# Paired heads of a hybrid attention block: product u is begun only behind the last matmul of product w

## The chip, the cores and the metric

The kernel runs on one core of a Trainium2 chip. The metric is the time on the device of one execution, in microseconds (us). Before the change it is 819.78 us, the median of three runs (819.44 to 820.15).

## What is computed

The reference is one decoder block on 512 tokens with a model width of 2048, in float32. The tokens are normalised and projected; two groups of heads attend in parallel, each head's output is gated, and one output projection and a last norm follow. Cut to what matters here:

```python
h = _rmsnorm(x, norm_g[l])
proj = h @ w_in[l]
(qa, kca, vca, ksa, vsa, kwa, vwa, za, ga, qb, kb, vb, zb) = jnp.split(proj, offsets, axis=-1)
...
o_a = gates[..., 0:1] * o_cmp + gates[..., 1:2] * o_sel + gates[..., 2:3] * o_win
y_a = o_a.reshape(B, S, WIDTH_A) * jax.nn.silu(za)
...
y_b = o_b.reshape(B, S, WIDTH_B) * jax.nn.silu(zb)
x = x + jnp.concatenate([y_a, y_b], axis=-1) @ w_out[l]
```

Group A has 8 heads of 128 (compressed, selected and window attention), group B 16 heads of 64 (a window of 128 with sinks). Each head of group A needs two projections of the same tokens: its query (out of qa) and its gate (out of za), each 2048 by 128.

## The kernel before

**Words.** TensorE multiplies float32 values as two words, a high word (whi, a copy by ScalarE) and a low word (wlo, the rest, a subtraction by VectorE). `mm3` (L121) makes three matmuls of each product: high by high (L122), high by low (L123), low by high (L124). A weight tile of 128 by 1024 is loaded by a DMA on SyncE's queue (raw), split by ScalarE (L634) and by VectorE (L635), and used by TensorE. In `mm3` as `prod` calls it, the third matmul is the first that reads the low words of the weights.

**Stages.** First the key and value projections with the compression of blocks (to about 180 us), then the heads of group A (to about 402 us), then the heads of group B, then the output projection with the norm. The change lies in the second stage.

**Paired heads.** Head 0 of group A is projected directly. For heads 1 to 7, `pair(h)` (L674) computes query and gate together in a scheme of seven products instead of eight: tokens are cut into two halves of 256, rows of the weights into even and odd blocks, and sums of weight tiles meet sums of token forms that were made earlier (`xf`, L621 to L631). The seven products are 22, p, 21, 12, w, u and q, in the order in which the code names them. Each is one call of `prod` (L661): eight blocks of the contraction, three matmuls of 128 by 256 each, so 24 matmuls. Two banks of PSUM take them (tile pj, names pa and pb): pa's first half takes p and then 12 on top, its second half w; pb's first half takes 22 and then 21, its second half u and then q. Between the products VectorE sums weight tiles (raw plus raw, L684 through `plus`), adds products to the running result (t or zr with pj, L684), and ScalarE copies a half out (L700, L706, L712). Once w and u are both added, VectorE turns the query by the rotary tables (L723 to L725), splits it (L486, L487) and attention can use it.

**Attention of a head.** `attn_a` (L534) goes through four blocks of 128 queries. For each a group of score matmuls (six or nine at L557) writes tile sp; sp has one buffer of three banks, so a group waits until VectorE has read the one before (L559, L563). ScalarE takes the exponentials (L569, L573) and scales (L583, L585), TensorE transposes (L595, L607, L609, tile tp, two buffers), the two engines split the result (L525, L526, and L613 to L615 for the last piece), and TensorE multiplies by the values (L601 to L603, L616, L618, tile op). VectorE gates the head's output (L498) and it is written away (tile yd, L500).

**Order.** A planner places the instructions of each engine when the program is built, by its own estimates, keeping data dependences. So the attention of one head and the products of the next are woven together on TensorE, and one engine's queue runs strictly in the built order. `tc.issue_after(i)` adds an order without data: what is named inside stands behind i on i's engine. `pair` uses it once (L697), for the sum of two weight tiles. Between w and u the code before prescribes nothing: they write different halves of different banks and read different weights (u1 and u5).

**Reloads.** At head 3 the keys and values of the second key head are fetched back into the tiles of the first (L764, L766). After head 7 the even blocks of the tokens are fetched back (L642), the rotary tables of group B replace those of group A in the same tiles (L778, L779) and are scaled by VectorE (L780, L781).

Of the kernel before, what the change touches and what calls it, by code (L numbers as in the profile page):

```python
# [35 lines left out]
def hybrid_block(ctx, tc, xT, xtm, w0, w1s, w2s, wz, wq, wkb, wo0, wos, cw1, cw2, cpos, rope, tabs, sinks, gT, fg, out):  # L36
# [34 lines left out]
    last = {}  # L71
# [47 lines left out]
    recent = {}  # L119

    def mm3(ps, ah, al, bh, bl, first, last, go_on=False):  # L121
        pe.matmul(ps, ah, bh, start=first, stop=False, skip_group_check=go_on)  # L122
        pe.matmul(ps, ah, bl, start=False, stop=False, skip_group_check=go_on)  # L123
        recent["mm"] = pe.matmul(ps, al, bh, start=False, stop=last, skip_group_check=go_on).ins  # L124
# [261 lines left out]
    for g in range(2):  # L386
        act.activation(KH[g][:, 0:CMP], kct[:, g * 32:g * 32 + 32], AF.Copy)
        dve.tensor_tensor(out=KL[g][:, 0:CMP], in0=kct[:, g * 32:g * 32 + 32], in1=KH[g][:, 0:CMP].bitcast(F32),
                          op=ALU.subtract)
# [271 lines left out]
    def prod(bank, u, op, new):  # L661
        for m in range(8):
            cs = slice(m * P, m * P + P)
            ah, al = xf[op, m]
            mm3(bank, u[0][:, cs], u[1][:, cs], ah, al, new and m == 0, m == 7, not new)

    tags = ["raw0", "raw1", "raw2", "raw3"]

# [5 lines left out]
    def pair(h, *early):  # L674
# [20 lines left out]
        with ExitStack() as behind:  # L695
            if "jj" in last:
                behind.enter_context(tc.issue_after(last["jj"]))  # L697
            plus(x2, x2, x4)
        prod(pb[:, H0], u0, "22", True)
        act.activation(d, pb[:, H0], AF.Copy, scale=-1.0)  # L700
        x3 = load(c3, 1)
        prod(pa[:, H0], u3, "p", True)
        plus(d, d, pa[:, H0])
        u2 = unit(x3)
        prod(pb[:, H0], u2, "21", False)
        act.activation(zr[:, H1], pb[:, H0], AF.Copy)  # L706
        plus(jj, d, zr[:, H1])
# [672 lines left out]
```

## Time and profile before

| what | before |
|---|---|
| time, median of three | 819.78 us |
| time of the profiled execution | 820.54 us |
| its span, first to last instruction | 818.8 us |
| instructions in it | 14134 |
| TensorE matmul, busy | 805.6 us (98%) |
| TensorE weight load, busy | 733.7 us (90%) |
| VectorE, busy | 666.6 us (81%) |
| ScalarE, busy | 483.6 us (59%) |
| mean granted clock of TensorE | 0.998 |

The profile calls the engines PE (matmul), PEld (weight load), DVE (VectorE), ACT (ScalarE), POOL and SP; a q behind a name is the engine's sequencer. A row of the timeline gives the start and the length in us, the engine, the line, the operation, the tile written and the tiles read, and in square brackets how long the engine had stood idle just before and which instruction ended that. A row of waits reads: who waited, for whom, us in total, how often, the longest. Matmul ends are modelled, so a matmul that waits shows as a hole before its weight load first.

### The profile page before, as it was taken

To read this page: it belongs to the slowest core of one execution; us is meant where nothing else is said; L and a number is where in the kernel's file an instruction comes from. 1 tells how busy PE (TensorE), PEld (TensorE's weight loads), DVE (VectorE), ACT (ScalarE), POOL (GpSimd) and SP (SyncE) were. 2 spreads that over 40 slices of the span, in tenths; PEclk is the share of its full clock that TensorE was granted. 3 is DMA by queue.
4 is the path that set the end of the run, shared out by engine and by line. 5 is a ranking of instruction groups with operands and counts; after the bars stand their busy time and mean duration, and the time that the engine had idled before them with its cause. 6 is when DMAs were issued, how large, how long until landed. Compare 5 with 4: busy or idle time off the path is not lost.

```text
span 818.8 us, 14134 instructions
## 1 busy us (share of the span) xinstructions
PE 805.6 (98%) x5281; PEld 733.7 (90%) x5281; DVE 666.6 (81%) x1326; ACT 483.6 (59%) x1026; POOL 67.7 (8%) x54
## 2 busy tenths in 40 slices
PE   9999999999999999999999999999999999999996
PEld 8888898999999999999988888888888888999996
DVE  7859786966889899899876688887687799777895
ACT  6734456564867687786756365645444657543545
POOL 4500002020000000000011211011001000000000
PEclk9999999999999999999999999999999999999999
DMA  9665786898421322423742422222222257497845
GB/s 327 201 204 168 264 289 226 258 333 306 137 85 33 116 78 93 168 83 99 233 141 68 138 78 55 75 87 69 78 78 77 77 145 260 145 244 205 242 99 205
DMA packets 52116, 128.30 MB, mean 157 GB/s; under 512 B 4944, under 2 KB 17232, under 8 KB 52048
## 3 DMA queue, kind: packets, MB, share of 16 engines
q1 hardware_dynamic: 50032, 120.59, 43.9%
q0 software_dynamic: 1728, 6.29, 4.4%
q8 instruction: 41, 0.67, 0.3%
q10 hardware_dynamic: 288, 0.52, 0.2%
q14 instruction: 27, 0.22, 0.1%
HBM read 110.31 MB, written 17.07 MB: 156 GB/s over the span
## 4 chain that ended last, share of the span: by engine, by line
PE 85%; DVE 5%; DMA 4%; ACT 3%; issue 2%; POOL 1%; SPq 0%; DVEq 0%; ACTq 0%; POOLq 0%
PE pj L124 16%; PE pj L123 16%; PE pj L122 16%; PE bank L124 4%; PE bank L122 4%; PE oa L123 4%; PE bank L123 4%; PE oa L122 4%; PE oa L124 3%; PE sp L557 3%; DMA rw<-wos 2%; PE tp L595 2%; PE tp L879 2%; DMA xr<-xT 1%; PE spb L844 1%
## 5 line engine op out<-in xcount | busy, mean ns | idle before, releaser
L124 PE MATMUL pj<-xh,wlo 128*128 128x512 f32 (+1 forms) x560 | 194.9, 348 | 1.8 <-DVE wlo L635 1.8
L122 PE MATMUL pj<-xh,whi 128*128 128x512 f32 (+1 forms) x560 | 194.7, 348 | 0.0
L123 PE MATMUL pj<-xl,whi 128*128 128x512 f32 (+1 forms) x560 | 194.6, 347 | 0.0
L96 DVE TENSOR_TENSOR wlo<-raw,whi 128x1024 fp32r<-128x1024 f32 (+2 forms) x102 | 116.7, 1148 | 34.8 <-ACT whi L95 29.4
L95 ACT ACTIVATE whi<-raw 128x1024 fp32r<-128x1024 f32 (+1 forms) x101 | 95.0, 943 | 76.9 <-PE pj L123 22.8
L124 PEld LDWEIGHTS pj<-xh,wlo 128*128 128x128 f32 x560 | 105.4, 188 | 15.0 <-DVE wlo L635 2.4
L123 PEld LDWEIGHTS pj<-xl,whi 128*128 128x128 f32 x560 | 105.3, 188 | 13.1 <-issue 0.9
L122 PEld LDWEIGHTS pj<-xh,whi 128*128 128x128 f32 x560 | 105.3, 188 | 12.2
L635 DVE TENSOR_TENSOR wlo<-raw,whi 128x1024 fp32r<-128x1024 f32 x49 | 59.5, 1220 | 9.3 <-ACT whi L634 9.2
L634 ACT ACTIVATE whi<-raw 128x1024 fp32r<-128x1024 f32 x49 | 51.1, 1054 | 21.1 <-DVE raw L684 6.1
L123 PE MATMUL oa<-wlo,yh 128*128 128x256 f32 (+1 forms) x168 | 50.2, 299 | 0.1
L122 PE MATMUL oa<-whi,yh 128*128 128x256 f32 (+1 forms) x168 | 49.8, 298 | 0.6 <-ACT yh L954 0.6
L124 PE MATMUL oa<-whi,yl 128*128 128x256 f32 (+1 forms) x168 | 49.5, 298 | 0.0
L858 ACT ACTIVATE ttb<-ttb,sums 128x256 f32<-128x256 f32 (+1 forms) x64 | 30.1, 471 | 26.5 <-DVE sums L851 26.1
L525 ACT ACTIVATE ph<-tp 128x512 fp32r<-128x512 f32 x56 | 32.4, 592 | 14.9 <-PE tp L595 8.7
L123 PE MATMUL bank<-wlo,xh 128*128 128x256 f32 (+1 forms) x128 | 40.3, 317 | 0.3 <-DVE wlo L96 0.3
L124 PE MATMUL bank<-whi,xl 128*128 128x256 f32 (+1 forms) x128 | 39.9, 314 | 0.0
L526 DVE TENSOR_TENSOR pl<-tp,ph 128x512 fp32r<-128x512 f32 x56 | 37.8, 684 | 1.9 <-ACT ph L525 1.8
L122 PE MATMUL bank<-whi,xh 128*128 128x256 f32 (+1 forms) x128 | 36.7, 318 | 1.5 <-ACT whi L95 1.5
L122 PE MATMUL bank<-xh,whi 128*128 128x512 f32 x96 | 37.3, 400 | 0.0
L123 PE MATMUL bank<-xl,whi 128*128 128x512 f32 x96 | 36.9, 389 | 0.0
L573 ACT ACTIVATE tt<-tt,sums 128x128 f32<-128x128 f32 (+3 forms) x64 | 35.3, 554 | 1.2 <-DVE sums L563 1.2
(359 smaller groups left out, 2172.6 us busy)
## 6 DMA issues: line engine op xcount, KB each, us to landing
raw<-wz SPq DMA_DIRECT2D x36, 512.0 KB, 3.6
raw<-wq SPq DMA_DIRECT2D x28, 512.0 KB, 3.7
raw<-cw SPq DMA_DIRECT2D x16, 512.0 KB, 4.6
raw<-wos SPq DMA_DIRECT2D x12, 512.0 KB, 4.6
rw<-wos SPq DMA_DIRECT2D x10, 512.0 KB, 5.6
xr<-xT SPq DMA_DIRECT2D x16, 256.0 KB, 5.0
raw<-w SPq DMA_DIRECT2D x8, 512.0 KB, 4.5
fd<-ft SPq DMA_DIRECT2D x4, 1024.0 KB, 6.2
```

The lines of the kernel that those rows point to most:

```text
L95: last["hi"] = act.activation(hi[:, :width], rw[:, :width], AF.Copy).ins
L96: last["lo"] = dve.tensor_tensor(out=lo[:, :width], in0=rw[:, :width], in1=hi[:, :width].bitcast(F32), op=ALU.subtract).ins
L122: pe.matmul(ps, ah, bh, start=first, stop=False, skip_group_check=go_on)
L123: pe.matmul(ps, ah, bl, start=False, stop=False, skip_group_check=go_on)
L124: recent["mm"] = pe.matmul(ps, al, bh, start=False, stop=last, skip_group_check=go_on).ins
L525: act.activation(ph, tp, AF.Copy)
L526: dve.tensor_tensor(out=pl, in0=tp, in1=ph.bitcast(F32), op=ALU.subtract)
L557: pe.matmul(sp[:, a:b], qq[:, qs], kk[0][:, ko:ko + b - a], start=pi == 0, stop=pi == 2)
L573: act.activation(tv, tv, AF.Exp, bias=mn[:, i, 1 + w:2 + w], scale=-1.0, accum_out=dn[:, i, 1 + w:2 + w])
L634: act.activation(hi, src, AF.Copy)
L635: last["lo"] = dve.tensor_tensor(out=lo, in0=src, in1=hi.bitcast(F32), op=ALU.subtract).ins
L858: act.activation(tv, tv, AF.Exp, bias=mn[:, e, v:v + 1], scale=-1.0, accum_out=dn[:, e, v:v + 1])
```

## The change

`prod` is the only place changed. While the first block of u is named (its first three matmuls), an order is in force that puts them on TensorE behind the last matmul of w, which `prod` notes down when it has named w. The blocks of u after the first are named outside that order; they add to the same half bank. It holds for the seven calls of `pair`. No tile, buffer, size or operation is changed.

```diff
         for m in range(8):
             cs = slice(m * P, m * P + P)
             ah, al = xf[op, m]
-            mm3(bank, u[0][:, cs], u[1][:, cs], ah, al, new and m == 0, m == 7, not new)
+            with ExitStack() as behind:
+                if m == 0 and op == "u":
+                    behind.enter_context(tc.issue_after(last["w"]))
+                mm3(bank, u[0][:, cs], u[1][:, cs], ah, al, new and m == 0, m == 7, not new)
+        if op == "w":
+            last["w"] = recent["mm"]
```

## The prediction

> **What bounds the kernel now.** I read the page first: busy shares, the slices, the chain that ended last.
>
> ```profile
> span 818.8 us, 14134 instructions
> PE 805.6 (98%) x5281; PEld 733.7 (90%) x5281; DVE 666.6 (81%) x1326; ACT 483.6 (59%) x1026; POOL 67.7 (8%) x54
> ...
> PE   9999999999999999999999999999999999999996
> ...
> PEclk9999999999999999999999999999999999999999
> ...
> PE 85%; DVE 5%; DMA 4%; ACT 3%; issue 2%; POOL 1%; SPq 0%; DVEq 0%; ACTq 0%; POOLq 0%
> ```
>
> TensorE (PE) bounds it, at full clock in every slice. The change keeps the number of matmuls and only moves them, so it can win no more than the time in which TensorE stands still, and only in the stage of the paired heads, where products w and u live. That stage runs from about 205 to 402 us. The view by windows gives the whole stage and two pieces of it.
>
> ```profile
> 205.00:402.00 197.00, 195.17 (x1611) 190.65 (x1611) 179.37 (x398) 147.82 (x364) 0.00 (x0) 1.00 0.33 107
> 308.00:338.00 30.00, 30.00 (x257) 29.80 (x256) 26.94 (x58) 21.82 (x54) 0.00 (x0) 1.00 0.46 160
> 338.00:368.00 30.00, 29.04 (x241) 28.32 (x241) 27.17 (x60) 23.71 (x59) 0.00 (x0) 1.00 0.19 62
> ```
>
> Columns: stretch, length, then busy time and count for PE, PEld (weight loads), DVE (VectorE), ACT (ScalarE). 257 matmuls in a stretch without a hole are 0.117 us each; the next stretch fits 16 fewer. VectorE is busy 179.37 of 197 us, 91%: it is the second bound. The time in which TensorE stands shows best on its weight loads, since matmul ends are modelled. Waits of PEld in the stage, and of PE behind it:
>
> ```profile
> PEld pj L124 <- DVE wlo L635: 2.4, 3, 1.2
> PEld tp L595 <- ACT tt L585: 0.9, 5, 0.2
> PEld op L616 <- DVE pcr L615: 0.4, 2, 0.2
> PEld sp L557 <- DVE ql L487: 0.3, 1, 0.3
> ...
> PE oa L122 <- ACT yh L954: 0.6, 1, 0.6
> ```
>
> Together 2.4 + 0.9 + 0.4 + 0.3 = 4.0 us. That is all that a better order could return. Behind the stage nothing but one wait of 0.6 us is named, so what the stage gains or loses goes through to the end nearly whole.
>
> [...] The named waits give 4.0, and the windows row without a hole still shows 0.2 us of PEld idle, so I go by the waits.
>
> **The change part by part.** It removes no instruction and adds none. One order is added on TensorE: the first three matmuls of u behind the last of w, in each of seven heads. In the built order before, u begins ahead of w in all seven, in pieces: in the first head 13 of its 24 matmuls ahead of a score group, 11 behind w. In the built order after, w is followed by u in all seven, and everything round them has been placed anew up to about 460 us; the tail is the same. So the sum is one over waits. The three large ones, all on the third matmul of product 22 of the next head, which needs the low words of the new weights:
>
> ```profile
> 220.69 0.39 PE L124 MATMUL pj<-xh,wlo 128*128 128x256 f32 x1 [0.32 <-DVE wlo L635]
> ...
> 251.19 0.39 PE L124 MATMUL pj<-xh,wlo 128*128 128x256 f32 x1 [0.52 <-DVE wlo L635]
> ...
> 341.12 0.39 PE L124 MATMUL pj<-xh,wlo 128*128 128x256 f32 x1 [0.96 <-DVE wlo L635]
> ```
>
> The loads ahead of them wait a little longer, 2.4 us in all. Why the low words are late:
>
> ```profile
> 218.24 0.28 PE L123 MATMUL pj<-pu,whi 128*128 128x256 f32 x1
> ...
> 219.42 0.28 PE L124 MATMUL pj<-pu,wlo 128*128 128x256 f32 x1
> 219.54 0.28 PE L122 MATMUL pj<-xh,whi 128*128 128x256 f32 x1
> ...
> 219.94 0.44 PE L595 MATMUL tp<-ident,tt 128*128 128x128 f32 x2
> ...
> 339.22 0.27 PE L607 MATMUL tp<-ident,tt 128*128 128x128 f32 x1
> ...
> 339.33 0.27 PE L595 MATMUL tp<-ident,tt 128*128 128x128 f32 x1
> ```
>
> *First head.* u ends at 219.5, two matmuls of 22 and two transposes follow, then TensorE waits for a split that VectorE began only at 219.41:
>
> ```profile
> 219.41 1.23 DVE L635 TENSOR_TENSOR wlo<-raw,whi 128x1024 fp32r<-128x1024 f32 x1 [0.43 <-ACT whi L634]
> ...
> 221.00 1.39 DVE L723 TENSOR_TENSOR t<-t,sinA 64x512 f32<-64x512 f32 x2
> ```
>
> After the change the same work lies ahead of u's end, so it stays near 219.5. Behind it the built order puts six transposes (339.33 - 339.22 = 0.11 each, 0.7) and the whole of q (24 x 0.117 = 2.8) before 22, whose third matmul then stands at about 223.3. VectorE adds u's result (0.4, from its end at 219.7), does the two sine products (1.4) and the split (1.2): ready at 222.7. No wait, with 0.6 us to spare.
>
> *Third head's 22.* Before, its split stands behind the reading of a score group, and VectorE lost 2.44 us ahead of that:
>
> ```profile
> 245.94 1.23 DVE L635 TENSOR_TENSOR wlo<-raw,whi 128x1024 fp32r<-128x1024 f32 x1 [2.44 <-ACT whi L634]
> ...
> 249.92 1.22 DVE L635 TENSOR_TENSOR wlo<-raw,whi 128x1024 fp32r<-128x1024 f32 x1
> ```
>
> After, the split stands ahead of that reading. From the end of the score group before to the third matmul of 22 TensorE has 51 product matmuls and nine score matmuls (1.44), 7.4 us; VectorE has one reading, a sum of 1.1, two splits of 1.14 and short rows, 5.4 us. No wait.
>
> *Sixth head's 22*, the largest:
>
> ```profile
> 336.73 0.42 DVE L684 TENSOR_TENSOR t<-t,pj 128x256 f32<-128x256 f32 x1 [1.12 <-PE pj L124]
> ...
> 336.87 0.64 PE L557 MATMUL sp<-KH,qh 128*128 128x288 f32 x3
> ...
> 338.51 0.19 DVE L559 CUSTOM_DVE_ANT_0 tc__3674<-sp,tab 128x32 f32<-128x32 f32 x1 [1.36 <-PE sp L557]
> ...
> 339.85 1.22 DVE L635 TENSOR_TENSOR wlo<-raw,whi 128x1024 fp32r<-128x1024 f32 x1
> ```
>
> VectorE idles 1.12 and 1.36 us for w's result and for a score group that stands behind 19 matmuls of u and all 24 of w, and the split slips by as much. After, that group stands ahead of both: 43 matmuls, 5.0 us, sooner. From it to 22's third matmul TensorE has 7.8 us of work, VectorE 5.8. No wait. So 2.4 us go. The high words that go ahead of each split come from ScalarE, 147.82 of 197 us busy; its queue, followed in the same way, has them ready at all three.
>
> Of the other 1.6 us (transposes waiting for scaled scores, the tail for its words) I can't name which stay: bounds 0 and 1.6 gone, half taken, 0.8.
>
> What is new: a score group waits until VectorE has read the one before, since there is one buffer for both.
>
> ```profile
> 212.68 0.64 PE L557 MATMUL sp<-KH,qh 128*128 128x288 f32 x3
> ...
> 214.12 0.28 PE L122 MATMUL pj<-xh,whi 128*128 128x256 f32 x1
> ...
> 236.26 0.18 DVE L559 CUSTOM_DVE_ANT_0 tc__2473<-sp,tab 128x32 f32<-128x32 f32 x1
> ...
> 236.72 0.42 DVE L563 CUSTOM_DVE_ANT_0 tt<-sp,tab 128x256 f32<-128x256 f32 x1
> ...
> 237.06 1.22 DVE L684 TENSOR_TENSOR raw<-raw 128x1024 f32<-128x1024 f32 x1
> ```
>
> Nine score matmuls take 214.12 - 212.68 = 1.44 us; reading a group of two 256-wide scans takes from 236.26 to 237.06, 0.8. In the built order after, only five product matmuls (0.6 us) stand between the second and third group of the second head, where before 41 matmuls stood; with 0.2 for the last matmul to drain that wait is 0.4 us if VectorE is free, 1.5 if it is one sum (1.14) behind. I take 0.4, since the queue ahead of it adds up to that moment, and 0.2 for waits of this kind that I don't see.
>
> On SyncE's queue the weight loads of later heads move past a head's write-back (four loads ahead of the first one instead of six).
>
> ```profile
> DMA to landing us min/median/max: 3.3/3.8/9.5
> ...
> DMA to landing us min/median/max: 5.5/5.9/6.3
> ```
>
> The first row is for the weights, the second for the reload of the values in the fourth head. In the stage no engine names a weight load as what it waited for. The reload had 15 us between the last reader and the next; after it has about 8, more than 6.3. I cost both at nothing; without that cover it is 1 or 2 us once.
>
> Sum: -2.4 - 0.8 + 0.4 + 0.2 = **-2.6 us**. The profiled execution took 820.54 us (span 818.8), 0.76 above the median of 819.78; the difference applied to it is 817.9, to the median **817.2**.
>
> **The rivals.** Told apart from no change is a difference of some 0.2%, 1.6 us.
>
> *The waits only move.* u begun early is a filler: in the fifth head its pieces stand between score groups and transposes. If that cover counts, the 1.6 us of transposes and tails double (+1.6) and the new score waits reach 1.0; with 2.4 gone that leaves +0.2, about 820. For it: VectorE is 91% busy, so a late split can turn up in front of another product. Against it: q and 22 take u's place as filler in the built order. [...] No row of before shows the cost of taking it out, so it stays here.
>
> *The score buffer becomes the bound: slower.* If VectorE runs one sum (1.14 us) later than I count, each of six heads pays that once at a score group: 6.8 - 4.0 = +2.8, about 822.6. It decides against the change from 4.0 / 6 = 0.7 us per head. For it: score groups stand closer together after. Against it: apart from the one place above I find 2 us or more between groups.
>
> *Sine rows.* In the last paired head the scaling of the next sine rows now stands ahead of the last step of that head's rotation, which waits with it.
>
> ```profile
> 408.65 0.69 DVE L781 TENSOR_TENSOR sinA<-sinA,rstdb 128x512 f32<-128x512 f32 x1 [1.40 <-DMA sinA<-rope]
> ...
> 409.72 0.69 DVE L487 TENSOR_TENSOR ql<-t,qh 128x512 fp32r<-128x512 f32 x1
> ...
> 412.81 0.29 PE L557 MATMUL sp<-KH,ql 128*128 128x288 f32 x1
> ```
>
> The query's low words (ql) already stood behind the scaling; the last step and the high words, some 0.7 each, now come between, so that ql ends near 411.8 in these times, 1.0 ahead of the score matmul at 412.81. The landing must slip by over 1 us before this costs anything, then it costs what it slips: at 2 us, 818.2, within the forecast.
>
> That the change doesn't do what it says is excluded: u follows w seven times in the built order.
>
> **How the numbers follow.** Forecast (1.6 to 4 us gained) 0.62, more than that 0.03, the waits only move 0.20, the score buffer 0.15. Faster 0.65, same 0.20, slower 0.15. The range reaches from all 4.0 us gone (815.8) to 1.0 us of net loss (820.8), which leaves out about half of the last rival.
>
> **What would show it.** In the changed profile the waits of L124 on L635 in the stage shrink from 2.4 to under 0.6; VectorE's 1.36 us ahead of a score group and 2.44 ahead of a split are gone; PEld waits come to about 1.4; transposes wait no more than 0.9. It is wrong if score matmuls (L557) name VectorE's scans (L563) for over 2 us in all, or if transposes and L616 wait over 2.5.

## The result and the profile after

| | before | after |
|---|---|---|
| median of six runs each | 820.34 us (819.44 to 822.12) | 816.54 us (815.67 to 817.95) |
| ratio, 95% interval | | 0.9951 (0.9937 to 0.9966) |
| profiled execution, its span | 820.54, 818.8 us | 816.30, 814.5 us |

The changed kernel is faster by 3.8 us, 0.5%, more than the 0.2% that can be told from no change; 816.5 stands beside a forecast of 817.2, which was worked out from a median of 819.78 us before; taken anew with the changed kernel, that median is 820.34. Lines of the changed kernel behind L665 are five higher than before: `plus` is L689, the rotation L728 to L730. The page, the parts that answer to those of before:

```profile
span 814.5 us, 14149 instructions
...
PE 801.4 (98%) x5281; PEld 731.2 (90%) x5281; DVE 665.3 (82%) x1326; ACT 486.9 (60%) x1026; POOL 64.8 (8%) x54
...
PE   9999999999999999999999999999999999999996
...
PEclk9999999999999999999999999999999999999998
...
PE 86%; DVE 5%; DMA 4%; ACT 2%; issue 2%; POOL 0%; SPq 0%; DVEq 0%; ACTq 0%; POOLq 0%
```

The page hardly moves: the same 5281 matmuls, TensorE still bounds. The view by windows, over the stage of the paired heads (which ends earlier now):

```profile
205.00:398.00 193.00, 192.25 (x1606) 189.66 (x1605) 177.49 (x397) 148.25 (x359) 0.00 (x0) 1.00 0.34 111
```

Matmuls stand for 0.75 us of it, where it was 1.83. What is left is named in the waits of the weight loads in the stage (195 to 425 us); these two rows are all:

```profile
PEld pj L122 <- DVE zr L689: 0.7, 2, 0.5
PEld sp L557 <- PE pj L124: 0.7, 1, 0.7
```

The 2.4 us of L124 for L635 are gone, and so are the 1.6 us of transposes (L595), tail (L616) and scores for the low query words. 1.4 us are new. First the three places of L124. TensorE:

```profile
222.55 0.28 PE L124 MATMUL pj<-xh,wlo 128*128 128x256 f32 x1
...
247.15 0.36 PE L124 MATMUL pj<-xh,wlo 128*128 128x256 f32 x1
...
329.31 0.73 PE L557 MATMUL sp<-KH,qh 128*128 128x288 f32 x3
...
331.53 0.37 PE L122 MATMUL pj<-xh,whi 128*128 128x256 f32 x1
...
338.78 0.36 PE L124 MATMUL pj<-xh,wlo 128*128 128x256 f32 x1
```

And VectorE:

```profile
220.56 2.36 DVE L635 TENSOR_TENSOR wlo<-raw,whi 128x1024 fp32r<-128x1024 f32 x2
...
243.54 2.36 DVE L635 TENSOR_TENSOR wlo<-raw,whi 128x1024 fp32r<-128x1024 f32 x2 [0.23 <-ACT whi L634]
245.83 0.18 DVE L559 CUSTOM_DVE_ANT_0 tc__2473<-sp,tab 128x32 f32<-128x32 f32 x1
...
331.50 0.18 DVE L559 CUSTOM_DVE_ANT_0 tc__3674<-sp,tab 128x32 f32<-128x32 f32 x1
...
336.44 1.22 DVE L635 TENSOR_TENSOR wlo<-raw,whi 128x1024 fp32r<-128x1024 f32 x1
```

None of the three third matmuls of product 22 carries a bracket. In the first head the split (first of the two from 220.56) is done by 221.8 and the matmul starts at 222.55. For the third head the split stands ahead of the reading of the score group at 245.83, not behind it. For the sixth head the score group starts at 329.31, ahead of the whole of w (from 331.53), VectorE reads it at 331.50 and has split by 337.7, 1.1 us before the matmul at 338.78.

Now the new stops. TensorE, then VectorE:

```profile
237.13 0.41 PE L557 MATMUL sp<-KH,ql 128*128 128x288 f32 x2
...
238.62 0.60 PE L557 MATMUL sp<-KH,qh 128*128 128x288 f32 x2 [0.48 <-DVE sums L563]
...
374.26 0.39 PE L122 MATMUL pj<-pu,whi 128*128 128x256 f32 x1 [0.27 <-DVE zr L689]
```

```profile
237.58 0.19 DVE L559 CUSTOM_DVE_ANT_0 tc__2473<-sp,tab 128x32 f32<-128x32 f32 x1 [0.21 <-PE sp L557]
...
372.49 1.19 DVE L635 TENSOR_TENSOR wlo<-raw,whi 128x1024 fp32r<-128x1024 f32 x1
...
373.78 0.42 DVE L689 TENSOR_TENSOR zr<-zr,pj 128x256 f32<-128x256 f32 x1
```

At 238.62 a score group waits for the reading of the one before, five product matmuls behind it; VectorE was free and had itself stood 0.21 us for that one. At 374.26 (and a shorter one near 315.6) product p of the next head waits until VectorE has added q of this head; that adding stands behind a split of 1.19 us. The two banks change places from head to head, so p goes into the bank whose other half holds q.

**Where the time went.** The build names the same matmuls in every plan, so two traces can be compared at points by which both have done the same set of them. Behind the common start of the stage the changed kernel is 0.9 us ahead by the end of the first head's reach (near 237 us), 1.4 by 268 us, 1.9 by 284 us and 3.8 by 373 us; behind the stage it stays between 3.5 and 3.7 us until 778 us of the kernel before, and 3.3 us are left near 800 us. The rest of the 4.2 us between the two profiled executions, 0.9 us, lies ahead of the stage, where the instructions are the same: over all the profiled executions below the stage starts anywhere between 195.4 and 197.2 us. So I compare the runs below from the start of the stage (the first matmul of head 1's product 22) to one and the same matmul near 800 us: 607.6 us before, 604.3 after. I call the difference from before the **progress**. One caution goes with it: from 722 us (of before) to that point all the kernels have the same order, and the progress still moves there, by 0.4 us in the changed kernel and by 0.0 to 0.8 us in the runs below. Differences of less than that between two rows of the table say nothing by themselves.

### The profile page after: what moved, and what is told of

It is laid out like the page before. It is cut to its first block, busy times and chain, and to the rows that moved or that the text cites. A ratio compares the mean times of both kernels' runs of the same rounds, so it can differ in the third digit from the quotient of the medians.

```text
span 814.5 us, 14149 instructions
## 1 busy us (share of the span) xinstructions
PE 801.4 (98%) x5281; PEld 731.2 (90%) x5281; DVE 665.3 (82%) x1326; ACT 486.9 (60%) x1026; POOL 64.8 (8%) x54
## 4 chain that ended last, share of the span: by engine, by line
PE 86%; DVE 5%; DMA 4%; ACT 2%; issue 2%; POOL 0%; SPq 0%; DVEq 0%; ACTq 0%; POOLq 0%
PE pj L123 16%; PE pj L122 16%; PE pj L124 16%; PE bank L124 4%; PE bank L122 4%; PE bank L123 4%; PE sp L557 4%; PE oa L123 3%; PE oa L122 3%; PE oa L124 3%; DMA xr<-xT 2%; DMA rw<-wos 2%; PE tp L595 2%; PE tp L884 2%; PE spb L849 1%
## 5 line engine op out<-in xcount | busy, mean ns | idle before, releaser
L122 PE MATMUL pj<-xh,whi 128*128 128x512 f32 (+1 forms) x560 | 194.8, 348 | 0.0
L124 PE MATMUL pj<-xh,wlo 128*128 128x512 f32 (+1 forms) x560 | 194.6, 347 | 0.0
L124 PEld LDWEIGHTS pj<-xh,wlo 128*128 128x128 f32 x560 | 105.3, 188 | 12.5 <-issue 0.2
L122 PEld LDWEIGHTS pj<-xh,whi 128*128 128x128 f32 x560 | 105.3, 188 | 12.1
L635 DVE TENSOR_TENSOR wlo<-raw,whi 128x1024 fp32r<-128x1024 f32 x49 | 59.4, 1219 | 7.0 <-ACT whi L634 6.8
L122 PE MATMUL oa<-whi,yh 128*128 128x256 f32 (+1 forms) x168 | 49.8, 298 | 0.6 <-ACT yh L959 0.6
L124 PE MATMUL oa<-whi,yl 128*128 128x256 f32 (+1 forms) x168 | 49.5, 298 | 0.0
L124 PE MATMUL bank<-whi,xl 128*128 128x256 f32 (+1 forms) x128 | 39.7, 312 | 0.0
L122 PE MATMUL bank<-whi,xh 128*128 128x256 f32 (+1 forms) x128 | 36.4, 316 | 1.3 <-ACT whi L95 1.3
L122 PE MATMUL bank<-xh,whi 128*128 128x512 f32 x96 | 36.7, 393 | 0.5 <-ACT whi L95 0.5
```

The source lines that it names most:

```text
L635: last["lo"] = dve.tensor_tensor(out=lo, in0=src, in1=hi.bitcast(F32), op=ALU.subtract).ins
```

## The experiments

The theory at the start: the gain is a sum of stops of TensorE taken out at their places, each where the next head's 22 waited for its low words. The rivals: weaving two products costs TensorE in itself; or what counts is the plan as a whole, which any added order lays anew. All twelve in one table; before was measured again with each of them, and the ratio is to that; "named" is the sum of TensorE's weight-load waits from 195 to 425 us (before 4.0, after 1.4). The diffs show the main lines; those of runs 1, 2 and 8 to 12 are against the changed kernel, those of runs 3 to 7 against the kernel before.

| run | median, us | ratio to before (95%) | named, us | progress, us |
|---|---|---|---|---|
| the change | 816.54 | 0.9951 (0.9937 to 0.9966) | 1.4 | -3.3 |
| 1 one head | 821.19 | 1.0001 (0.9990 to 1.0012) | 3.7 | +0.3 |
| 2 first head | 821.14 | 0.9997 (0.9987 to 1.0007) | 4.2 | +0.9 |
| 3 22 behind q | 825.49 | 1.0057 (1.0037 to 1.0078) | 8.5 | +6.2 |
| 4 u ahead of w | 822.73 | 1.0028 (1.0014 to 1.0042) | 6.0 | +2.0 |
| 5 score group, head 5 | 827.18 | 1.0078 (1.0064 to 1.0091) | 9.3 | +6.6 |
| 6 score group, all | 821.82 | 1.0014 (1.0005 to 1.0022) | 6.0 | +2.0 |
| 7 u and 22 | 818.08 | 0.9974 (0.9965 to 0.9983) | 1.2 | -1.8 |
| 8 split behind q | 817.65 | 0.9965 (0.9952 to 0.9978) | 0.9 | -3.2 |
| 9 two stops out | 817.06 | 0.9959 (0.9947 to 0.9971) | 1.3 | -2.9 |
| 10 woven, last head | 818.20 | 0.9966 (0.9955 to 0.9978) | 2.4 | -2.7 |
| 11 woven, all | 827.91 | 1.0095 (1.0079 to 1.0112) | 9.5 | +6.5 |
| 12 one stop out | 816.54 | 0.9947 (0.9933 to 0.9960) | 1.0 | -3.6 |

**1. One head.** The change in head 5 alone, at whose end the longest stop lay; `last["h"]` holds the head that `pair` builds.

```diff
-                if m == 0 and op == "u":
+                if m == 0 and op == "u" and last["h"] in (5,):
```

> Only in head 5 is product u begun behind the last matmul of w; the order of every other head's instructions is that of the kernel before. Theory (the gain is a sum of waits of TensorE taken out spot by spot, each where product 22 of the next head waited for its low words): the wait of 1.1 us at 341 us, for head 6's product 22, goes, and nothing else: 1.3 to 1.5 us below the kernel before, near 818.9 us; the waits at 220.7 and 251.2 us stand. Rival 'weaving two products costs TensorE in itself': a seventh of the stage's gain of 3.6 us, 0.5 us. Rival 'the gain is in the re-laid plan of the whole stage': nothing, within 0.3 us of the kernel before.

The order on TensorE is that of before but for 46 rows, in which w now stands whole ahead of u. Nothing is won. VectorE, and TensorE behind it (the lines here are one higher than in the changed kernel):

```profile
336.00 0.41 DVE L690 TENSOR_TENSOR t<-t,pj 128x256 f32<-128x256 f32 x1
339.19 0.19 DVE L559 CUSTOM_DVE_ANT_0 tc__3674<-sp,tab 128x32 f32<-128x32 f32 x1 [2.77 <-PE sp L557]
...
340.53 1.22 DVE L635 TENSOR_TENSOR wlo<-raw,whi 128x1024 fp32r<-128x1024 f32 x1
```

```profile
337.55 0.64 PE L557 MATMUL sp<-KH,qh 128*128 128x288 f32 x3
...
341.81 0.39 PE L124 MATMUL pj<-xh,wlo 128*128 128x256 f32 x1 [0.96 <-DVE wlo L635]
```

w's result is there at once now (VectorE's wait of 1.12 us for it is gone), but the score group still stands behind 43 matmuls of both products, so VectorE stands 2.77 us in front of it, where it stood 1.12 + 1.36 before, and the stop of 0.96 us is the same to the hundredth. My theory missed here by its whole 1.3 to 1.5 us: u behind w doesn't take this stop out. The rival of weaving, 0.5 us, finds no support in the trace either. The third rival, that the gain is in a plan laid anew, expected nothing here, and nothing came.

**2. First head.** The same edit with `in (1,)`.

> Only in head 1 is u begun behind w; the first head then goes as in the changed kernel, and the heads behind it are laid otherwise than in either kernel, with u woven into w again in most of them. Theory: the wait of 0.8 us at 220.7 us goes (1.05 us in the progress of TensorE), and the new wait for the score group near 238 us comes (0.65 to 0.86); what the other heads give is read from the waits that they show, and the sum of holes between weight loads must give the time within 0.5 us. Rival 'weaving costs in itself': 0.5 us below the kernel before, whatever the waits. Rival 'any re-laid plan': most of the 3.6 us.

The first spot comes out as in the changed kernel, 0.9 us ahead by 225 us and 1.4 by 268 us. Then the newly laid third and fourth head lose it: transposes wait 2.3 us for scaled scores, and behind that TensorE runs at half its clock (third number from the end of a row: PEclk).

```profile
PEld tp L595 <- ACT tt L585: 2.3, 2, 1.4
```

```profile
290.00:291.00 1.00, 0.32 (x3) 0.31 (x3) 0.97 (x4) 1.00 (x3) 0.00 (x0) 0.57 0.00 0
291.00:292.00 1.00, 1.00 (x7) 1.00 (x5) 1.00 (x7) 1.00 (x3) 0.00 (x0) 0.50 0.00 0
292.00:293.00 1.00, 1.00 (x7) 1.00 (x6) 1.00 (x3) 1.00 (x5) 0.00 (x0) 0.50 0.00 0
293.00:294.00 1.00, 1.00 (x8) 1.00 (x8) 1.00 (x2) 1.00 (x6) 0.00 (x0) 0.72 0.54 33
```

0.43 + 0.50 + 0.50 + 0.28 = 1.7 us of full clock lost, which no wait names. So this spot was worth what the theory says, and the plan behind it took it back. The waits (0.2 above before) and the half clock add up to +1.9 us, the progress is +0.9: the sum was expected to hold within 0.5 us and misses by 1.0.

**3. 22 behind q.** u is free; the next head's 22 stands behind the last of q.

```diff
+                if m == 0 and op == "22" and "q" in last:
+                    behind.enter_context(tc.issue_after(last["q"]))
...
+        if op == "q":
+            last["q"] = recent["mm"]
```

> Product u is left free, woven with w as before; instead product 22 of each next head is begun only behind the last matmul of product q of the head ahead. Theory: what made the waits was that 22 came ahead of its low words, not that u and w were woven: the three waits at L124 for the low words of L635 (2.4 us named, 2.6 with the restarts) go, so 2.4 to 3.5 us below the kernel before, 816.8 to 817.9 us. Rival 'weaving u into w costs TensorE in itself': no gain, within 0.5 us of the kernel before. Rival 'the half banks': q and then 22 wait for VectorE's reading, over 1 us of waits at L122, and the time stays within 1 us of the kernel before.

All waits of L124 on L635 are gone, as the theory wanted, and the kernel is nearly 5 us slower: other products and the transposes wait instead.

```profile
PEld tp L595 <- ACT tt L585: 4.4, 6, 1.4
PEld pj L122 <- DVE t L689: 1.6, 2, 1.3
PEld sp L557 <- DVE ql L487: 0.8, 2, 0.6
```

8.5 us named, 4.5 more than before, and 1.7 us of half clock near 295 us come to the 6.2 us of progress lost. So taking the three stops at L124 out doesn't by itself win their time.

**4. u ahead of w.** The two products whole and one behind the other, in the other order: `pair` names u ahead of w, and w's first three matmuls stand behind the last of u.

> The two products are whole and one behind the other, as in the change, but in the other order: u first, w only behind u's last matmul. Rival 'weaving costs in itself': the same gain as the change, 3.6 us in the stage, near 816.6 us. Theory (only the waits count): the gain is what is left of the waits; product q lies ahead of the next 22 in most heads here too, so 1.5 to 3.6 us below the kernel before, and the sum of holes between weight loads gives it within 0.5 us. Rival 'w has to come first, since its sum is wanted first': 1 us or more slower than the kernel before, with waits that name the half bank of w.

2 us slower. The wait at L124 is 0.2 us; what came is this:

```profile
PEld pj L122 <- ACT t L705: 2.6, 4, 1.2
PEld sp L557 <- ACT tt L573: 1.6, 1, 1.6
```

The first is a product that waits for ScalarE's copy out of its bank; the second is one stop, which the matmuls' own waits put down to the reload of the keys (`DMA KH<-Kd`, 1.5 us). The waits of 6.0 us, 2.0 more than before, are the 2.0 us lost. Two products with nothing of one woven into the other, and no gain: the rival that weaving costs TensorE in itself, which expected the gain of the change here, falls.

**5 and 6. The score group ahead of both.** With run 1 in hand the theory took a second form: what held the sixth head's split was the fourth score group standing behind both products. w and u are left free toward each other and begun only behind that group, in head 5 alone (run 5) or in every head (run 6).

```diff
-                        pe.matmul(sp[:, a:b], qq[:, qs], kk[0][:, ko:ko + b - a], start=pi == 0, stop=pi == 2)
+                        last["sp"] = pe.matmul(sp[:, a:b], qq[:, qs], kk[0][:, ko:ko + b - a], start=pi == 0, stop=pi == 2).ins
...
+                if m == 0 and op in ('w', 'u') and last["h"] in (5,):
+                    behind.enter_context(tc.issue_after(last["sp"]))
```

> Order between w and u is free. Instead, in head 5 alone, both are begun only behind the fourth score group (nine matmuls, L557) of the attention of head 4. Up to that place the order is that of the kernel before, behind it the plan is laid anew. Theory, second form (the wait for head 6's product 22 came from the score group standing behind 43 product matmuls, so that VectorE read it late and split late): the stop of 1.35 us near 341 us goes, TensorE's progress at head 6's product p is 1.1 to 1.5 us ahead of the kernel before; the end is that, plus or minus the stops that the newly laid heads 6 and 7 show. Rival 'only u being whole behind w does it': the stop stays, as in the run of one head.

> Order between w and u is free (u comes in pieces ahead of and between w in most heads). In every head both are begun only behind the fourth score group of the attention of the head ahead. Theory, second form: no stop at L124 for L635 is left, so at least the changed kernel's gain of 2.4 us if no new stops come; what comes new is score groups (six and nine matmuls) that stand with few or no matmuls between them and wait for VectorE's reading, about 0.6 us each where they touch (two heads here): 816.5 to 818.5 us. Rival 'the plan decides by chance': new stops of other kinds over 2.5 us, no gain or a loss.

In run 5 the order is that of before up to head 5, and then the fourth group follows the third with nothing between:

```profile
331.80 0.53 PE L557 MATMUL sp<-KH,ql 128*128 128x288 f32 x2
334.70 0.60 PE L557 MATMUL sp<-KH,qh 128*128 128x288 f32 x2 [2.37 <-DVE sums L576]
```

```profile
331.27 0.69 DVE L498 SCALAR_TENSOR_TENSOR st<-op,st 128x512 f32<-128x512 f32 x1 [0.18 <-PE op L618]
331.88 1.22 DVE L688 TENSOR_TENSOR raw<-raw 128x1024 f32<-128x1024 f32 x1
...
333.41 0.18 DVE L559 CUSTOM_DVE_ANT_0 tc__3674<-sp,tab 128x32 f32<-128x32 f32 x1
```

VectorE reaches the reading of the third group only at 333.41, behind the gate and a sum of weights, so the one score buffer comes free late and TensorE stops 2.8 us, twice what was to be won. The long stop for the sixth head's low words is gone, but the kernel is 6.6 us behind at the end (waits 5.3 us above before, half clock once). Run 6 has the same illness in a milder form: 5.7 of its 6.0 us are score groups waiting. Both expected gains missed. In the changed kernel the same two groups have 12 product matmuls, the tail and a transpose between them.

**7. u and 22.** The change and run 3 together.

```diff
+    ahead = {"u": "w", "22": "q"}
...
+                if m == 0 and op in ahead and ahead[op] in last:
+                    behind.enter_context(tc.issue_after(last[ahead[op]]))
...
+        last[op] = recent["mm"]
```

> The change, and besides it product 22 of the next head is begun only behind the last matmul of q; heads 4 to 7 then come out alike. Theory: no stop at L124 for L635; the half bank of q is read by VectorE before 22 and p need theirs only if its queue is early, so stops at L122 for L689 may come; if they don't, up to 1.4 us below the changed kernel (815 us); from the run with 22 behind q alone, whose stops came from transposes that waited for scaled scores when q was no longer their cover, 2 to 4 us above the changed kernel. I lean to the second. Rival 'less weaving is better': below the changed kernel.

Faster than before, 1.5 us slower than the change; only two stops are named.

```profile
PEld sp L557 <- PE pj L124: 0.7, 1, 0.7
PEld op L602 <- DVE pl L526: 0.5, 1, 0.5
```

1.2 us, 0.2 less than in the changed kernel, and yet 1.5 us less progress. The difference builds up in pieces of 0.4 us and less between 255 and 373 us; the wait of L602 is one of them, the views give the others no name, and it stays open. Order between products alone, in two places, is no better than in one.

**8, 9 and 12. Single stops taken out of the changed kernel.** Run 8: in head 7, VectorE splits product 21's weights only behind its adding of q. Run 12: in head 2, the fifth block of product 12 stands behind the second score group, so that 12 and not 5 product matmuls separate it from the third. Run 9, whose diff is shown: both. `last["sp", 1]` holds the last matmul of the second score group, `last["qadd"]` VectorE's adding of q.

```diff
+                if m == 4 and op == "12" and last["h"] in (2,):
+                    behind.enter_context(tc.issue_after(last["sp", 1]))
...
-        u2 = unit(x3)
+        u2 = words(STILL)
+        act.activation(u2[0], x3, AF.Copy)
+        with ExitStack() as behind:
+            if h == 7:
+                behind.enter_context(tc.issue_after(last["qadd"]))
+            last["lo"] = dve.tensor_tensor(out=u2[1], in0=x3, in1=u2[0].bitcast(F32), op=ALU.subtract).ins
```

> The change, and in head 7 alone the low words of product 21's weights are split by VectorE only behind its adding of q of head 6. All is laid as in the changed kernel up to the score group ahead of head 7's product p. Theory: the stop of 0.57 us near 374 us goes, nothing else until there: 0.3 to 0.6 us below the changed kernel, near 816.1 us, unless the last head, laid anew, stops elsewhere. Rival 'such a stop costs nothing, the time is made up later': the same as the changed kernel within 0.2 us, though the stop is gone.

> The changed kernel with two of its three stops taken out one by one: in head 2 product 12 is begun with four blocks only behind the second score group of the attention ahead (its fifth block), so that 12 and not 5 product matmuls stand between the second and the third group; and in head 7 the split of product 21 as in the run before of that name. Else all is laid as in the changed kernel up to the last paired head. Theory (the time is the sum of TensorE's stops at given spots): the stop of 0.77 us near 238 us goes, 0.6 us, and stays won to the end; with the 0.14 us that were left at the end in the run with the split alone, 0.7 to 0.8 us below the changed kernel. Rival 'what is won at one spot is lost at the next wait': the stop goes and 0.2 us or less is left at the end.

> The changed kernel with only the order in head 2 from the run with two stops out (12 and not 5 product matmuls between the second and the third score group); all the rest of the order on TensorE is that of the changed kernel to the end. Theory: the stop near 238 us shrinks as it did there, by 0.3 us, and since nothing behind is laid anew the 0.3 us stay won through the next stage to the end of the profiled execution (the medians can't tell 0.3 us apart). Rival 'lost at the next wait': under 0.1 us left behind 430 us.

Up to the places edited, matmuls in these traces start at the times of the changed kernel to 0.02 us, less the offset from the early stage, so single stops can be followed. Run 8: its stop near 374 us is gone, 0.46 us ahead by 378 us; the last head, laid anew, gives 0.3 back by 435 us. That is less than the 0.3 to 0.6 us expected at the end. Run 9: 0.3 us ahead behind 238 us, 0.7 from 381 to 409 us, and 0.0 from 429 us on, so the expected 0.7 to 0.8 us missed and the rival's number came. Where it is lost, this appears:

```profile
423.71 0.33 PE L595 MATMUL tp<-ident,tt 128*128 128x128 f32 x1 [0.26 <-ACT tt L585]
```

Run 12, in which nothing behind head 2 is laid anew, is 0.31 us ahead at 239 us and 0.34 us at 559 us, and no less than 0.31 at any point up to 791 us. So what a stop gives back is kept over 550 us if the order behind it stays; in runs 8 and 9 it goes where the plan is laid anew. To the very end it was not kept. Near 791 us a wait for low words is 0.3 us shorter in run 12 (0.61 us ahead), but its last 130 matmuls follow each other at 0.118 us where every other trace here has 0.113, and 0.05 us are left at the last one. Why is open; the progress of -3.6 in the table lies on that slope. The stop itself only shrank from 0.7 to 0.3 us though 12 matmuls stand in the gap: VectorE, in whose queue a sum of weights now stands ahead, reads the group before it only from 237.84 us, and that sets it. Run 12 is the best kernel found; its median is that of the change (816.54 us), which the runs can't tell from 0.3 us less.

**10 and 11. Strictly woven.** The opposite of the change: w and u in turns of three matmuls, in head 7 of the changed kernel (10) or in all seven heads (11). `block` is one turn of the loop of `prod`.

```diff
+        if h in (7,):
+            u5 = unit(x2)
+            for m in range(8):
+                for out, words2, op in ((pa, u1, "w"), (pb, u5, "u")):
+                    with ExitStack() as behind:
+                        if (m, op) != (0, "w"):
+                            behind.enter_context(tc.issue_after(recent["mm"]))
+                        block(out[:, H1], words2, op, True, m)
+            plus(d, d, pa[:, H1])
```

> The changed kernel, but in head 7 w and u are strictly alternated, three matmuls of each in turn; up to there all is laid as in the changed kernel, and the last score group stands in the same place. Theory (the order between w and u is worth nothing in itself): TensorE's progress behind the last of both products is that of the changed kernel within 0.1 us, and the end within 0.5 us. Rival 'weaving costs TensorE': 0.5 us lost already behind the last of both.

> w and u strictly alternated, three matmuls of each in turn, in all seven heads: the opposite of the change; the plan is laid anew from head 1 on, and q comes out whole ahead of the next 22 in nearly all heads. Theory: no stop at L124 for L635, since q stands ahead of 22; gain or loss is decided by the stops that show (w's result comes 2.7 us later, and VectorE's queue with it): sign open, the sum of stops gives the stage within 0.7 us. Rival 'weaving costs': at least as slow as the kernel before.

Run 10 shows what weaving costs TensorE in this head: from the start of both products to their last three matmuls it loses 0.00 us against the changed kernel. Then it loses 1.04 us within 7 us:

```profile
397.98 0.42 DVE L692 TENSOR_TENSOR t<-t,pj 128x256 f32<-128x256 f32 x1 [0.98 <-PE pj L124]
```

```profile
398.54 0.47 PE L122 MATMUL pj<-xh,whi 128*128 128x512 f32 x1 [0.26 <-DVE t L692]
...
399.41 0.38 PE L601 MATMUL op<-ph,VH 128*128 128x256 f32 x1 [0.17 <-ACT ph L525]
```

In the changed kernel, VectorE added w early, and stood 0.93 us in front of its next instruction:

```profile
391.16 0.41 DVE L689 TENSOR_TENSOR t<-t,pj 128x256 f32<-128x256 f32 x1
```

Woven, w ends with u, VectorE stands 0.98 us for it, the next product waits for the bank, and the split of the transposed scores and with it L601 come later. Here weaving costs through what waits for the first product's result. It misses both expectations in part: no loss on TensorE's own account, but 1.0 us at the end where I had allowed 0.5. Run 11 is the slowest of all, as the rival of weaving expected (no faster than before), with 9.5 us of waits of eight kinds and half clock once; one of the waits is the reload of the values, which nothing covers there:

```profile
PEld op L603 <- DMA VL<-Vd: 1.4, 1, 1.4
```

**What follows from the twelve.** The sum of TensorE's named waits plus the half clock gives the progress within 1.1 us in every run, over a spread of 10 us: with the waits less those of before, for instance, +4.5 + 1.7 for run 3 (measured +6.2), +2.0 for runs 4 and 6 (+2.0 each), -3.1 for run 8 (-3.2), -2.6 for the change (-3.3). That part of the theory stands, to about that 1 us. The other part, that the change takes stops out by the order of w and u, falls at the longest stop: put in there with the plan round it left as it was, the order is worth nothing (run 1). At the other two stops the order could not be tried without a new plan. What the change does is to make the planner lay the heads anew, and that plan has few stops; other added orders (runs 2 to 7 and 11) led to plans from 1.8 us better to 6.6 us worse than before. Why the planner's estimates lead to a good plan here and to bad ones there was not tried.

## Why the prediction was right, and where it was not

- **TensorE bounds, and no more than 4.0 us can be won.** Right for the change, which won 3.3 to 3.8 us. As a bound 4.0 us isn't strict: run 12 is 4.0 us ahead at 722 us and still shows 1.0 us of named waits. The weight loads of the stage are busy 189.66 of 193.00 us now, 3.34 us short, while 1.4 us of waits are left (197.00 - 190.65 = 6.35 us short before, with 4.0 us of waits). So the idle time of the weight loads overstated the room that the named waits give, before and after, by 2.4 and 1.9 us.
- **-2.4 us, the three stops at L124.** Right, at all three places and in the way that was read from the built order (split ahead of the reading; score group ahead of both products; q and transposes between u and 22). Two counts were off without harm: eight transposes, not six, stand between u and q in the first head, and the new order differs from the old up to 544 us, not 460. Named waits understate it a little: the longest counted 1.16 us, while the loads around it started 1.35 us apart instead of 0.12.
- **-0.8 us, half of the other waits.** Wrong in size: all 1.6 us went. This is the first mis-sized term, a half taken between two bounds.
- **+0.4 us, the score buffer.** The right place (where 43 matmuls stood before, not 41); 0.5 us by the matmul, 0.7 by its weight load, with VectorE free, as assumed. The 0.2 us for the last matmul to drain is what the rows show from the start of the next matmul to VectorE's reading: 338.51 - 338.31 before, 237.58 - 237.38 after. Run 12 shows the other case: with the group before done earlier, VectorE was not free, and 0.3 us stayed.
- **+0.2 us, waits not seen.** Wrong in size and kind: 0.7 us at L122, product p waiting for the bank that holds q. The prediction did not follow who reads that bank before p may write into it.
- **The sum, -2.6.** By the same view it is -2.4 - 1.6 + 0.7 + 0.7 = -2.6 us: 0.8 us more won and 0.8 us more lost than forecast, which cancelled by luck. Measured from the start of the stage it is 3.7 us by 561 us of the kernel before (3.3 near 800 us, by the medians 3.8). Up to there the weight loads stand idle 2.9 us less (364.04 - 334.85 us before, 360.37 - 334.11 after), somewhat more than the names add up to, and the same loads are busy 0.7 us less; why they take less is open. The forecast of 817.2 lies as near as it does also because the median that it started from was 0.6 us low.
- **Reloads and the sine rows, at nothing.** Right in the changed kernel, where no engine waits for either on TensorE's behalf. The price put on a lost cover, 1 or 2 us once, is what runs 4 and 11 paid (1.5 and 1.4 us).
- **The rival "the waits only move".** Given 0.20 and not what happened, yet it is what happened to runs 3, 5, 6 and 11: waits at L124 gone or fewer, and others in their place. In the changed kernel q and 22 took the place of the early u, and taking it out of the mix cost nothing.
- **The signs it named.** The waits of L124 on L635 went from 2.4 us to none that is named, the weight loads' waits came to 1.4 us, as said, and no transpose is named. VectorE's 1.4 us in front of the sixth head's score group became 0.4, but it stands 1.1 to 1.3 us in front of one in three other heads, without a wait of TensorE behind it.
- **What the prediction left out** is the difference between the plan and the edit. It read the new plan spot by spot, and that gave the right answer; its reasons would have been wrong for the edit by itself, as run 1 shows at the longest stop.

## What to carry to other kernels

When a planner orders the instructions, an added order is worth what the plan it leads to is worth: build it, compare the plans spot by spot, and sum TensorE's waits, and don't credit the order itself until it has been put in where nothing else moves. A stop taken out where all behind it stays in place was kept over 550 us (0.31 us at the place, 0.34 us at 559 us); where the rest is laid anew it may be lost within one head. When two products are woven, look at who waits for the first result: in run 10 weaving cost TensorE nothing while it multiplied and 1.0 us through VectorE, which got the first result later. Finishing one before the other is no gain by itself (runs 1 and 4).

## What was not expected of the hardware

**The granted clock dropped behind broken stops.** In run 2 three stops of 0.46, 1.58 and 1.12 us within 3.3 us (287.53 to 290.69, from one matmul's start to the next's), with a few matmuls between, were followed by a granted clock of 0.50, which took 1.7 us more. Runs 3, 5 and 11 show the same once each: 0.15 + 0.50 + 0.50 + 0.50 + 0.05 = 1.70 us of full clock lost in run 3 (293 to 298 us), 0.32 + 0.50 + 0.50 + 0.38 = 1.70 in run 5 (335 to 339 us), 0.14 + 0.50 + 0.50 + 0.50 = 1.64 in run 11 from 323 to 327 us, where the view ends. Behind other stops the clock stayed at 1.00. Run 5, the drop and then stops near 384 us with none behind them:

```profile
331.00:334.00 3.00, 1.33 (x9) 0.90 (x7) 2.82 (x11) 0.90 (x2) 0.00 (x0) 1.00 0.98 307
334.00:335.00 1.00, 0.30 (x2) 0.33 (x3) 1.00 (x6) 1.00 (x5) 0.00 (x0) 1.00 0.98 387
335.00:336.00 1.00, 1.00 (x6) 0.86 (x5) 0.77 (x1) 1.00 (x6) 0.00 (x0) 0.68 1.05 416
336.00:337.00 1.00, 1.00 (x6) 0.91 (x5) 0.00 (x0) 1.00 (x5) 0.00 (x0) 0.50 0.97 328
...
384.00:387.00 3.00, 1.17 (x6) 0.48 (x4) 3.00 (x4) 3.00 (x6) 0.00 (x0) 1.00 0.99 310
387.00:388.00 1.00, 0.75 (x5) 0.56 (x6) 1.00 (x8) 1.00 (x4) 0.00 (x0) 1.00 0.75 289
388.00:389.00 1.00, 1.00 (x9) 1.00 (x9) 1.00 (x2) 1.00 (x3) 0.00 (x0) 1.00 0.04 14
```

And stops of run 6, with 1.00 over its whole stage:

```profile
270.00:272.00 2.00, 1.38 (x9) 0.96 (x7) 2.00 (x8) 0.91 (x2) 0.00 (x0) 1.00 0.72 288
272.00:273.00 1.00, 0.01 (x1) 0.04 (x1) 1.00 (x6) 1.00 (x4) 0.00 (x0) 1.00 0.70 133
273.00:274.00 1.00, 1.00 (x6) 0.92 (x7) 1.00 (x1) 1.00 (x5) 0.00 (x0) 1.00 0.79 319
```

Matmuls were busy for 1.33 of 3.00 us ahead of the drop in run 5 and for 1.65 of 3.00 us (287 to 290 us) in run 2; they were busy for 1.17 of 3.00 us in run 5 from 384 us and for 1.39 of 3.00 us in run 6 from 270 us, with no drop behind. Ends of matmuls are modelled, but by these figures busy time over such a stretch doesn't tell the two kinds apart; what sets the drop was not shown.

**Traces repeat to hundredths.** Where runs 8 and 12 have the order of the changed kernel, matmuls start within 0.02 us of each other's times over 170 us and more (0.1 us in run 1 against before), behind an offset from the early stage that varies by 1.8 us from one execution to the next. Within this stage, differences of 0.3 us, far below what medians show, can be read from one profile each; behind 722 us they can't, by the caution above.
